# A two-layer encoder trunk: another order for the gate stage and the query and key projections, and feed-forward work moved to GpSimd

## The chip, the cores and the metric

The kernel runs on one core of one Trainium2 chip. The metric is the device time of one launch in microseconds. Before the change the median of three runs is 1855.73 us (1855.55 to 1857.43).

TensorE (PE in the profile, PEld for its weight loads) multiplies matrices and writes only to PSUM, eight banks of 128 x 512 fp32. VectorE (DVE), ScalarE (ACT) and GpSimd (POOL) do the elementwise work; each of them takes its instructions strictly in the order in which they were queued. SyncE (SP) issues most DMAs, also in order.

## The reference, cut to what matters

Two requests (512 prompt tokens and 256 sample tokens) go through DEPTH = 2 layers with the same weights. A layer is a mixer and a convolutional gated feed-forward network, each followed by a residual sum and a layer norm:

```python
aq, ak, av, lq, lk, lv, lo, lg = _split_cols(x @ w_in)
att = _head_rmsnorm(_diff_attention(aq, ak, av, lam), att_g) * (1.0 - lam_init)
gates = lg + gate_bias            # log input and forget gates, forward and backward
h = _mlstm(q, k, v, ig_f, lf_f) + flipped _mlstm(..., ig_b, lf_b)
mixed = concat([att, sigmoid(lo) * _head_rmsnorm(h, lstm_g)])
x = _layer_norm(ALPHA * x + mixed @ w_out)
gate, up = split(x @ w_gu)        # 2816 columns each
conv = conv_b + sum(gp[:, j:j + S] * conv_w[j] for j in range(3))
x = _layer_norm(ALPHA * x + (gelu(conv) * up) @ w_down)
```

Everything is fp32. The mLSTM needs, per head and direction, running sums and running maxima over the tokens of its gates, and exponentials of them, before it can form any state.

## The kernel before, in words

The 768 tokens are six tiles of 128; tiles 0 and 1 are the sample, tiles 2 to 5 the prompt. Activations lie transposed in `actA`, each value split into a high and a low part. A product takes three passes over the parts (`PASSES`), so one 128 x 512 output tile over 1024 inputs is 24 matmuls. Weights come by DMA into six raw buffers (`_load`, L140), ACT makes the high part (L171) and DVE the low part (L172), into 12 slots (`Weights`). `take` hands out the next block, `done` gives its slot back and plans the next conversion.

**Order of the work.** Python generators write the instructions down. `weave` (L739) advances several generators in turn: it always picks the one with the smallest (steps done + 0.5) / n, where n is the number given beside it. The place at which an instruction is written is its priority; a planner then fills each engine's queue. At every moment of its own estimate it takes the instruction of highest priority that it believes ready. So a matmul written early can stand behind later ones in the queue if the planner thought its inputs late. On the chip the queue is kept as it is: an instruction at its head whose input is late holds up all behind it.

**Gates, per layer.** After `lstm_in`, `gates()` (L428) runs beside `dense("av")`, the value projection of the attention (six tiles of 24 matmuls). Its chain: logarithms on DVE and ACT up to `gs` (L461), transposes `gT` on PE (L474), scans on DVE (L483 to L487), sums and differences, an exponential on ACT (L509) and one of a small tile `ae` (L514), a product `aB` of `ae` on PE (L517), and four groups of transposes `colT` (L524). Two of its results go through DRAM (`scr_m`, `scr_e`) and come back broadcast over all partitions: `lstm_decay` loads `pt` (L570), adds a mask on DVE (L572) and takes exponentials on ACT (L574).

**Query and key projections.** `att_in(h)` (L666) takes two weight blocks each for the query and the key of a head. `feat_major` (L347) runs 24 weight tiles; for each it multiplies the sample's 256 tokens into `psB` and the prompt's 512 into `psA`. Query and key of one head share the PSUM bank `aqkB` for the sample. Then ACT and DVE split the result into `sQ` (L678 to L681) or `sK` and `kL` (L683 to L688). `att(h)` (L692) does the scores (L708, L709), softmax and value product, sample first for heads 0 to 2. The value projection of the mLSTM, `dense("lv")`, is woven with `att(0)`.

**Feed-forward.** The 22 feature tiles (`ff_tile`, L924) use a scheme of seven products instead of eight (`product`, 12 matmuls of 384 columns each; p1, p2, p4, p6, p7, p5, p3 in this order). It needs four combinations of weight tiles, T1 to T4: T1 = u0 - g0 and T3 = u1 - u0 on GpSimd, T2 = u1 - T1 and T4 = T2 - g1 on VectorE (L149, planned at L299 to L302); each has one buffer, which becomes free when its conversion is done. The seven PSUM results are combined by DVE into the gate half `g` and the `up` half; the convolution, GELU and product with `up` (L954 to L964) follow. After the first tile of a group, `down` (L966) multiplies the three (last: four) tiles of the group before with `w_down`, in two PSUM banks by turns, and DVE adds each result to `acc` (L988). There are seven groups per layer; the last `down` uses three other banks.

Of the kernel before, what the change touches and what calls it, by code (L numbers as in the profile page):

```python
# [13 lines left out]
F32 = mybir.dt.float32  # L14
F32R = mybir.dt.float32r
AF = mybir.ActivationFunctionType
ALU = mybir.AluOpType
# [3 lines left out]
SA, SB = 512, 256  # L21
T = SA + SB
# [11 lines left out]
HALF = T // 2  # L34
# [12 lines left out]
PR_A = 0  # L47
PR_L = 0
PR_LO = 10
# [156 lines left out]
def trunk(ctx, nc, tc, d, o, depth=DEPTH):  # L206
    V, S, G, PE = nc.vector, nc.scalar, nc.gpsimd, nc.tensor
# [18 lines left out]
    def P(tag, name):  # L226
        return pp.tile([128, 512], F32, tag=tag, name=name, bufs=banks[tag])

    actA = cp.tile([128, 8, 2, T], F32R, name="actA")
# [17 lines left out]
    for i in range(2):  # L247
        k = 4 * i
# [17 lines left out]
    for l in range(depth):  # L266
        if l:
            for u in range(4):
                W.unit(d["w_c1"][l, u], 1056)
        for u in range(4):  # L270
            W.unit(d["w_av"][l, u])
        for h in range(4):
            W.unit(d["w_aq"][l, h])
            W.unit(d["w_ak"][l, h])
            if h == 0 or h == (1 if L1 else 2):
                for u in range(4):
                    W.unit(d["w_lv" if h == 0 else "w_lo"][l, u])
        for hf in range(2):
            for u in range(4):
                W.unit(d["w_out"][l, hf, u])  # L280
        early = {}
        for i in range(FF_EARLY):
            early[i] = [W.piece(d["w_g"][l, i, :, p * 512:(p + 1) * 512], 512) for p in range(2)]
            for src in early[i]:
                W.block(src, 512)
        for kind, i in ffn_seq:
            if kind == "f":

                def half(w, p):
                    return W.piece(d[w][l, i, :, p * 512:(p + 1) * 512], 512)  # L290

                if i in early:
                    g0, g1 = early[i]
                else:
                    g0, g1 = half("w_g", 0), None
                u0, u1 = half("w_u", 0), half("w_u", 1)
                if g1 is None:
                    g1 = half("w_g", 1)
                t1 = {"a": u0, "b": g0, "tag": "T1", "engine": G}  # L299
                t2 = {"a": u1, "b": t1, "tag": "T2", "engine": V}  # L300
                t3 = {"a": u1, "b": u0, "tag": "T3", "engine": G}
                t4 = {"a": t2, "b": g1, "tag": "T4", "engine": V}  # L302
                for src in (t4, t2, t3, t1, u1) if i in early else (g0, g1, t4, t2, t3, t1, u1):
                    W.block(src, 512)
            else:
                f0, f1 = FF_GROUPS[i]
                for hf in range(2):
                    for f in range(f0, f1):
                        W.block(W.piece(d["w_down"][l, f, :, hf * 512:(hf + 1) * 512], 512), 512)
# [29 lines left out]
    PASSES = ((0, 0), (0, 1), (1, 0))  # L339
# [6 lines left out]

    def feat_major(blocks, psA, psB):  # L347

        n = 0
        for k in range(8):  # L350
            _, h, l = blocks[k // 4]
            for a, b in PASSES:
                w = (h, l)[a][:, (k % 4) * 128:(k % 4 + 1) * 128]
                PE.matmul(psB, w, actA[:, k, b, 0:SB], start=n == 0, stop=n == 23)  # L354
                PE.matmul(psA, w, actA[:, k, b, SB:T], start=n == 0, stop=n == 23)  # L355
                n += 1

    def transposed_split(src, name, tag, hi, lo):

# [8 lines left out]
    for l in range(depth):  # L368
# [3 lines left out]
        av = ra.tile([128, NT, 512], F32, name="av")  # L372
# [24 lines left out]
        def dense(tag, evac):  # L397
            units = [W.take() for _ in range(8)]
            for t in range(NT):
                p = P("d", f"{tag}{t}")  # L400
                tok_major(t, units, p, slice(0, 512))
                evac(t, p)
                yield
            W.done(*units)
# [23 lines left out]
        def gates():  # L428
            GP = ExitStack()
            gp = GP.enter_context(tc.tile_pool(name=f"gp{l}", bufs=1, reuse_waits="tile"))  # L430
            t1 = gp.tile([128, T], F32, name="t1")
# [5 lines left out]
            for di in range(2):  # L437
                for pr in range(2):
                    for hh in range(2):
                        s = sel[:, di * 2 + pr, hh * 64:(hh + 1) * 64]  # L440
                        G.affine_select(out=s, in_=s, pattern=[[0, 64]], compare_op=ALU.not_equal, fill=1.0, base=-(di * 32 + pr * 2 + hh), channel_multiplier=1)
            f = gt[:, :, :, 1, :]
            g1 = gp.tile([128, NT, 2, 4], F32, name="g1")
# [12 lines left out]
                                   in1=g1.rearrange("p a b c -> p (a b c)"), op0=ALU.add, op1=ALU.subtract)  # L456
# [10 lines left out]
            t2 = gp.tile([128, T], F32, name="t2")  # L467
            mpe = gp.tile([64, 2, 6], F32, name="mpe")
            ae = gp.tile([64, 6], F32, name="ae")
            for c0, c1 in ((0, 4), (4, 6)):  # L470
                ps = P(TAG_GT, f"gT{c0}")
                n = (c1 - c0) * 128
                for t in range(c0, c1):
                    PE.transpose(ps[:, (t - c0) * 128:(t - c0 + 1) * 128], gs[:, t].rearrange("p a b c -> p (a b c)"), ident)  # L474
                S.copy(ig[:, c0 * 128:c1 * 128], ps[0:64, :n])
                V.tensor_copy(lf[:, c0 * 128:c1 * 128], ps[64:128, :n])
# [35 lines left out]
            V.tensor_tensor(out=v6(t2[64:128]), in0=v6(t1[0:64]), in1=me.unsqueeze(2).to_broadcast([64, 6, 128]), op=ALU.subtract)  # L512
            V.tensor_tensor(out=ae, in0=mp, in1=me, op=ALU.subtract)
            S.activation(ae, ae, AF.Exp)  # L514
            ps = P(TAG_GT, "aB")
            for i in range(4):
                PE.matmul(ps[:, i * 6:(i + 1) * 6], sel[:, i, :], ae, start=True, stop=True)  # L517
# [221 lines left out]
        def weave(*gens):  # L739

            live = [[0, n, i, g, (*o, 0)[0]] for i, (g, n, *o) in enumerate(gens)]
            while live:
                e = min(live, key=lambda e: ((e[0] + 0.5) / e[1], e[2]))
                e[0] += 1
                with prio(e[4]):
                    done = next(e[3], live) is live
                if done:
                    live.remove(e)

        def chain(*gens):  # L750
            for g in gens:
                yield from g
# [3 lines left out]
            late_constants()  # L756
        G.iota(dneg, [[-1, 896]], base=384, channel_multiplier=1, allow_small_or_imprecise_dtypes=True)
        V.scalar_tensor_tensor(out=dneg, in0=dneg, scalar=-1.0, in1=dneg, op0=ALU.mult, op1=ALU.min)
        weave((gates(), 8), (dense("av", ev_av), 7))
        CPX = ExitStack()  # L760
        lc = CPX.enter_context(tc.tile_pool(name=f"lc{l}", bufs=1, reuse_waits="tile"))
        weave((att_in(0), 3))
        weave((att(0), 7, PR_A), (dense("lv", ev_lv), 7, PR_LO))
        lo = dense("lo", ev_lo)
        weave((chain(att_in(1), att(1)), AT1, PR_A), (chain(lstm_states(lc), *[lstm_out(lc, c) for c in range(OUTS)]), 4 * OUTS + 9, PR_L), *([(islice(lo, L1), L1 + W1)] if L1 else []))
        weave((chain(att_in(2), att(2)), AT2, PR_A), (chain(*[lstm_out(lc, c) for c in range(OUTS, NT)]), 4 * (NT - OUTS) + 1, PR_L), *([(islice(lo, L2), L2 + W2, PR_LO)] if L2 else []))
# [157 lines left out]
        def ff_tile(f):  # L924
            w0, w1, w2, cb = (convw[:, l, f, i:i + 1] for i in range(4))
            g = ft.tile([128, T], F32, tag="g", name=f"g{f}")
            up = ft.tile([128, T], F32, tag="up", name=f"up{f}")
            c = ft.tile([128, T], F32, tag="c", name=f"c{f}")
            m1, u2, u3, u4 = (ft.tile([128, HALF], F32, tag=t, name=f"{t}_{f}") for t in ("m1", "u2", "u3", "u4"))
            lo_, hi_ = slice(0, HALF), slice(HALF, T)  # L930
            p1 = bank(f"p1_{f}")
            product(p1, A11)
            S.copy(m1, p1)
            p2 = bank(f"p2_{f}")
            product(p2, A12)
            yield
            V.tensor_tensor(out=g[:, lo_], in0=p2, in1=m1, op=ALU.add)
            p4 = bank(f"p4_{f}")
            product(p4, A22)
            p6 = bank(f"p6_{f}")  # L940
            product(p6, S2)
            V.tensor_tensor(out=u2, in0=p6, in1=m1, op=ALU.add)
            p7 = bank(f"p7_{f}")
            product(p7, S3)
            V.tensor_tensor(out=u3, in0=p7, in1=u2, op=ALU.add)
            V.scalar_tensor_tensor(out=g[:, hi_], in0=p4, scalar=-1.0, in1=u3, op0=ALU.mult, op1=ALU.add)  # L946
            p5 = bank(f"p5_{f}")
            product(p5, S1)
            V.tensor_tensor(out=u4, in0=p5, in1=u2, op=ALU.add)
            V.tensor_tensor(out=up[:, hi_], in0=p5, in1=u3, op=ALU.add)  # L950
            p3 = bank(f"p3_{f}")
            product(p3, S4)
            V.tensor_tensor(out=up[:, lo_], in0=p3, in1=u4, op=ALU.add)
            S.activation(c, g, AF.Identity, bias=cb, scale=w1)  # L954
            for a, b in ((0, SB), (SB, T)):
                V.scalar_tensor_tensor(out=c[:, a + 1:b], in0=g[:, a:b - 1], scalar=w0, in1=c[:, a + 1:b], op0=ALU.mult, op1=ALU.add)
                V.scalar_tensor_tensor(out=c[:, a:b - 1], in0=g[:, a + 1:b], scalar=w2, in1=c[:, a:b - 1], op0=ALU.mult, op1=ALU.add)
            S.activation(c, c, AF.Gelu)
            V.tensor_tensor(out=up, in0=up, in1=c, op=ALU.mult)
            s = f % RING  # L960
            for half, sl in ((0, lo_), (1, hi_)):
                hi, lo = hm_half(s, 0, half), hm_half(s, 1, half)
                S.activation(hi, up[:, sl], AF.Identity)
                V.tensor_tensor(out=lo, in0=up[:, sl], in1=hi.bitcast(F32), op=ALU.subtract)  # L964
# [133 lines left out]
```

## Time and profile before

| | before |
|---|---|
| median of 3 runs | 1855.73 us |
| profiled execution | 1855.45 us, span 1853.7 us |
| granted TensorE clock, mean | 0.992 |
| PE busy | 1804.3 us (97%) |
| DVE, ACT, POOL busy | 1340.4 us (72%), 768.9 us (41%), 241.9 us (13%) |
| gate stage and first head, layer 1 | about 45 to 117 us of the span |
| the same, layer 2 | about 967 to 1036 us |
| feed-forward, layers 1 and 2 | about 436 to 904 us, 1355 to 1810 us |

The span runs from the first to the last instruction. Busy time is summed by engine; a wait is the idle time of an engine just before an instruction, put down to what released it. A granted clock of 1.00 is 2.4 GHz, one of 0.50 is 1.2 GHz.

### The profile page before, as it was taken

What the parts mean: (1) busy time and instruction counts of PE and PEld (TensorE: products, weight loads), DVE (VectorE), ACT (ScalarE), POOL (GpSimd) and SP (SyncE); (2) the same over time, 40 slices, a digit from 0 to 9 for tenths busy, and PEclk for the clock granted to TensorE, in tenths of its full rate; (3) what the DMA queues carried; (4) which work ended last, traced back from release to release, by engine and by line L of the source; (5) the groups of instructions that cost most, each with busy time, mean ns of one, the idle gap of its engine ahead of it and who ended that gap; (6) DMA issues with size and microseconds to landing.
All of it is one profiled execution on the core that took longest, in us unless ns stands there. A gap on an engine that the chain in (4) does not pass through costs nothing.

```text
span 1853.7 us, 26256 instructions
## 1 busy us (share of the span) xinstructions
PE 1804.3 (97%) x9692; PEld 1587.1 (86%) x9692; DVE 1340.4 (72%) x2576; ACT 768.9 (41%) x1624; POOL 241.9 (13%) x260
## 2 busy tenths in 40 slices
PE   8899999999999999999998999999999999999998
PEld 8778777789899899899897787777898998998996
DVE  5434787589887786787954457775898877877878
ACT  4344576425343343343332455672353343343340
POOL 2000111041111111110120011011411111111102
PEclk9999999999999999999999999999999999999999
DMA  6232110402322222122322121104022221221211
GB/s 190 67 79 69 35 58 24 159 18 69 92 74 69 64 74 68 64 75 86 101 96 83 42 69 52 46 25 170 2 90 80 80 79 47 80 76 51 80 63 68
DMA packets 83280, 134.95 MB, mean 73 GB/s; under 512 B 7984, under 2 KB 27056, under 8 KB 83152
## 3 DMA queue, kind: packets, MB, share of 16 engines
q1 hardware_dynamic: 82432, 132.90, 22.7%
q8 instruction: 76, 1.25, 0.3%
q14 instruction: 52, 0.43, 0.1%
q10 hardware_dynamic: 720, 0.37, 0.1%
HBM read 126.86 MB, written 6.39 MB: 72 GB/s over the span
## 4 chain that ended last, share of the span: by engine, by line
PE 78%; DVE 13%; ACT 5%; issue 2%; POOL 2%; DMA 1%; SPq 0%; DVEq 0%; ACTq 0%; POOLq 0%
PE p L921 32%; PE dn L981 16%; PE wo L877 5%; PE aqkA L355 3%; PE lv L345 3%; PE lo L345 3%; PE aqkB L354 2%; DVE wl L172 2%; PE c1a L345 2%; PE u L724 2%; PE av L345 2%; PE c1b L345 2%; PE num L618 1%; ACT wh L171 1%; PE num L614 1%
## 5 line engine op out<-in xcount | busy, mean ns | idle before, releaser
L921 PE MATMUL p<-actA,wh 128*128 128x384 f32 x1408 | 363.4, 338 | 3.2 <-DVE g L946 3.2
L171 ACT ACTIVATE wh<-raw 128x512 fp32r<-128x512 f32 (+1 forms) x348 | 215.5, 629 | 303.3 <-PE p L921 110.2
L172 DVE TENSOR_TENSOR wl<-raw,wh 128x512 fp32r<-128x512 f32 (+1 forms) x348 | 243.2, 708 | 96.9 <-ACT wh L171 96.4
L921 PE MATMUL p<-actB,wh 128*128 128x384 f32 x1056 | 270.0, 337 | 0.0
L921 PEld LDWEIGHTS p<-actA,wh 128*128 128x128 f32 x1408 | 254.7, 188 | 5.8 <-DVE g L946 3.8
L921 PE MATMUL p<-actA,wl 128*128 128x384 f32 x704 | 237.3, 337 | 0.0
L149 POOL TENSOR_TENSOR T<-raw,raw 128x512 f32<-128x512 f32 x88 | 120.5, 1371 | 837.0 <-DVE wl L172 525.7
L981 PE MATMUL dn<-wh,actB 128*128 128x512 f32 x576 | 208.8, 396 | 1.1 <-DVE acc L988 1.1
L171 ACT ACTIVATE wh<-T 128x512 fp32r<-128x512 f32 x176 | 108.4, 628 | 221.3 <-DVE acc L988 104.9
L921 PEld LDWEIGHTS p<-actB,wh 128*128 128x128 f32 x1056 | 191.3, 188 | 0.0
L981 PE MATMUL dn<-wh,ring 128*128 128x512 f32 x480 | 179.1, 396 | 1.6 <-DVE acc L988 1.6
L921 PE MATMUL p<-actB,wl 128*128 128x384 f32 x528 | 177.2, 336 | 0.0
L988 DVE TENSOR_TENSOR acc<-acc,dn 128x512 f32<-128x512 f32 x144 | 98.1, 681 | 72.0 <-PE dn L981 71.7
L172 DVE TENSOR_TENSOR wl<-T,wh 128x512 fp32r<-128x512 f32 x176 | 129.6, 748 | 22.0 <-ACT wh L171 21.9
L981 PEld LDWEIGHTS dn<-wh,actB 128*128 128x128 f32 x576 | 108.0, 188 | 29.8 <-DVE acc L988 2.8
L921 PEld LDWEIGHTS p<-actA,wl 128*128 128x128 f32 x704 | 132.2, 188 | 0.1
L877 PE MATMUL wo<-wh,actB 128*128 128x512 f32 x384 | 122.7, 396 | 0.0
L981 PE MATMUL dn<-wl,actB 128*128 128x512 f32 x288 | 113.2, 393 | 0.0
L981 PEld LDWEIGHTS dn<-wh,ring 128*128 128x128 f32 x480 | 90.0, 188 | 24.6 <-DVE acc L988 4.2
L921 PEld LDWEIGHTS p<-actB,wl 128*128 128x128 f32 x528 | 99.1, 188 | 0.0
L355 PE MATMUL aqkA<-actA,wh 128*128 128x512 f32 x256 | 98.8, 408 | 0.0
L981 PE MATMUL dn<-wl,ring 128*128 128x512 f32 x240 | 94.5, 394 | 0.0
(265 smaller groups left out, 3412.5 us busy)
## 6 DMA issues: line engine op xcount, KB each, us to landing
raw<-in_w_g_dram SPq DMA_DIRECT2D x88, 256.0 KB, 2.8
raw<-in_w_u_dram SPq DMA_DIRECT2D x88, 256.0 KB, 2.8
raw<-in_w_down_dram SPq DMA_DIRECT2D x88, 256.0 KB, 2.8
raw<-in_w_out_dram SPq DMA_DIRECT2D x32, 256.0 KB, 2.6
pt<-scr_m SPq DMA_DIRECT2D x12, 512.0 KB, 6.2
raw<-in_w_c_dram SPq DMA_DIRECT2D x16, 264.0 KB, 3.6
raw<-in_w_av_dram SPq DMA_DIRECT2D x16, 256.0 KB, 4.1
raw<-in_w_aq_dram SPq DMA_DIRECT2D x16, 256.0 KB, 3.7
```

The lines of the kernel that those rows point to most:

```text
L149: src["engine"].tensor_tensor(out=src["tile"], in0=a, in1=b, op=ALU.subtract)
L171: self.nc.scalar.activation(h, v, AF.Identity)
L172: self.nc.vector.tensor_tensor(out=l, in0=v, in1=h.bitcast(F32), op=ALU.subtract)
L345: PE.matmul(ps, xh(k, t, a), (h, l)[b][:, cols], start=k + i == 0, stop=k == 7 and i == 2)
L354: PE.matmul(psB, w, actA[:, k, b, 0:SB], start=n == 0, stop=n == 23)
L355: PE.matmul(psA, w, actA[:, k, b, SB:T], start=n == 0, stop=n == 23)
L614: PE.matmul(pn[:, di * 256:di * 256 + 129], qet[r, di, hh // 2, :], cst[di, c][r, hh // 2, :], start=di == dirs[0], stop=False, skip_group ...
L724: PE.matmul(pu[:, qt * 128:(qt + 1) * 128], aT[:, st * 128:(st + 1) * 128], av[:, s0 + st, h * 128:(h + 1) * 128], start=st == 0, stop=st ...
L877: PE.matmul(p, actB[:, k, a, t * 128:(t + 1) * 128], units[k][1 + b], start=n + i == 0, stop=n == 7 and i == 2)
L921: PE.matmul(ps, blk[1 + a][:, k * 128:(k + 1) * 128], x[:, k, b, :], start=k + i == 0, stop=k == 3 and i == 2)
L981: PE.matmul(p, x, (wh_, wl_)[b], start=k + i == 0, stop=k == nf - 1 and i == 2)
L988: V.tensor_tensor(out=z, in0=z, in1=p, op=ALU.add)
```

## The change

Four edits. (1) `gates()` gets two more yields, before the `gT` transposes and before the `aB` product, and is woven in ten steps with a longer chain: the value projection, `att_in(0)`, and the first tile of `lv`. The separate step for `att_in(0)` goes, and `att(0)` is woven with the five tiles of `lv` that remain. (2) `feat_major` does all 24 matmuls of the sample, then all 24 of the prompt; this holds for all four heads. (3) T2 and T4 are computed on GpSimd. (4) In `ff_tile` ACT copies p5 to the SBUF tile `m5`, and GpSimd adds it to `u2` (in place) and to `u3` (into the second half of `up`), where DVE did both from PSUM.

```diff
-                t2 = {"a": u1, "b": t1, "tag": "T2", "engine": V}
+                t2 = {"a": u1, "b": t1, "tag": "T2", "engine": G}
                 t3 = {"a": u1, "b": u0, "tag": "T3", "engine": G}
-                t4 = {"a": t2, "b": g1, "tag": "T4", "engine": V}
+                t4 = {"a": t2, "b": g1, "tag": "T4", "engine": G}
...
-        n = 0
-        for k in range(8):
-            _, h, l = blocks[k // 4]
-            for a, b in PASSES:
-                w = (h, l)[a][:, (k % 4) * 128:(k % 4 + 1) * 128]
-                PE.matmul(psB, w, actA[:, k, b, 0:SB], start=n == 0, stop=n == 23)
-                PE.matmul(psA, w, actA[:, k, b, SB:T], start=n == 0, stop=n == 23)
-                n += 1
+        for ps, tok in ((psB, slice(0, SB)), (psA, slice(SB, T))):
+            n = 0
+            for k in range(8):
+                _, h, l = blocks[k // 4]
+                for a, b in PASSES:
+                    w = (h, l)[a][:, (k % 4) * 128:(k % 4 + 1) * 128]
+                    PE.matmul(ps, w, actA[:, k, b, tok], start=n == 0, stop=n == 23)
+                    n += 1
...
             ae = gp.tile([64, 6], F32, name="ae")
+            yield
             for c0, c1 in ((0, 4), (4, 6)):
...
             S.activation(ae, ae, AF.Exp)
+            yield
             ps = P(TAG_GT, "aB")
...
-        weave((gates(), 8), (dense("av", ev_av), 7))
+        lv = dense("lv", ev_lv)
+        weave((gates(), 10), (chain(dense("av", ev_av), att_in(0), islice(lv, 1)), 10))
         CPX = ExitStack()
         lc = CPX.enter_context(tc.tile_pool(name=f"lc{l}", bufs=1, reuse_waits="tile"))
-        weave((att_in(0), 3))
-        weave((att(0), 7, PR_A), (dense("lv", ev_lv), 7, PR_LO))
+        weave((att(0), 7, PR_A), (lv, 6, PR_LO))
...
-            V.tensor_tensor(out=u4, in0=p5, in1=u2, op=ALU.add)
-            V.tensor_tensor(out=up[:, hi_], in0=p5, in1=u3, op=ALU.add)
+            S.copy(m5, p5)
+            G.tensor_tensor(out=u2, in0=m5, in1=u2, op=ALU.add)
+            G.tensor_tensor(out=up[:, hi_], in0=m5, in1=u3, op=ALU.add)
...
-            V.tensor_tensor(out=up[:, lo_], in0=p3, in1=u4, op=ALU.add)
+            V.tensor_tensor(out=up[:, lo_], in0=p3, in1=u2, op=ALU.add)
```

## Rows read from the trace of the kernel before

**Rows 1.** The page, part 1: busy time of each engine, share, instructions.
```profile
PE 1804.3 (97%) x9692; PEld 1587.1 (86%) x9692; DVE 1340.4 (72%) x2576; ACT 768.9 (41%) x1624; POOL 241.9 (13%) x260
```

**Rows 2.** PE's waits, whole span: instruction <- releaser: total us, times, longest us.
```profile
PE aB L517 <- ACT ae L514: 10.5, 2, 5.3
...
PE aqkB L354 <- DVE sQ L681: 5.8, 2, 3.4
PE p L921 <- DVE g L946: 3.2, 2, 1.6
PE dn L981 <- DVE acc L988: 2.7, 10, 0.3
...
PE s L708 <- ACT sK L685: 1.8, 2, 0.9
```

**Rows 3.** Timeline of PE, both layers' gate stages: start, us, instruction, [idle before <- releaser].
```profile
45.19 0.40 PE L345 MATMUL av<-wh,actA 128*128 128x512 f32 x1
...
50.55 0.63 PE L474 MATMUL gT<-ident,gs 128*128 128x128 f32 x4 [0.80 <-DVE gs L461]
...
67.11 1.84 PE L517 MATMUL aB<-ae,sel 64*128 64x6 f32 x8 [5.26 <-ACT ae L514]
...
966.81 0.39 PE L345 MATMUL av<-wh,actA 128*128 128x512 f32 x1
...
973.25 0.63 PE L474 MATMUL gT<-ident,gs 128*128 128x128 f32 x4 [1.16 <-DVE gs L461]
...
989.80 1.84 PE L517 MATMUL aB<-ae,sel 64*128 64x6 f32 x8 [5.25 <-ACT ae L514]
```

**Rows 4.** Windows: length, then busy of PE, PEld, DVE, ACT, POOL; PEclk; DMA share; GB/s.
```profile
67.10:73.00 5.90, 5.89 (x19) 5.00 (x20) 0.18 (x1) 0.31 (x1) 0.00 (x0) 0.51 0.02 6
...
104.30:108.00 3.70, 3.66 (x14) 3.38 (x15) 3.27 (x5) 1.82 (x5) 0.00 (x0) 0.50 0.09 8
108.00:117.00 9.00, 8.86 (x41) 7.13 (x40) 2.23 (x4) 6.05 (x16) 0.00 (x0) 0.86 0.23 77
...
989.80:995.00 5.20, 5.20 (x19) 4.54 (x20) 0.18 (x1) 0.77 (x2) 0.00 (x0) 0.55 0.02 5
...
1024.80:1028.00 3.20, 3.19 (x13) 2.97 (x14) 2.84 (x5) 1.79 (x5) 0.00 (x0) 0.57 0.01 4
```

**Rows 5.** Chain of work that ended last: start, us, piece (24 and 252 matmuls).
```profile
73.28 5.55 PE av L345 x24
...
500.30 43.97 PE p L921 x252
```

**Rows 6.** The same chain, then ACT's timeline, from 93 to 103 us.
```profile
93.04 7.22 DMA pt<-scr_m
...
101.16 1.57 ACT L574 ACTIVATE pt<-pt,cols 128x128 f32<-128x128 f32 x5 [5.72 <-DVE pt L572]
102.64 0.36 ACT L678 ACTIVATE sQ<-aqkB 64x256 fp32r<-64x256 f32 x1
```

**Rows 7.** Groups by line and shape, 500 to 904 us: busy us, mean ns | idle before.
```profile
L172 DVE TENSOR_TENSOR wl<-raw,wh 128x512 fp32r<-128x512 f32 x87 | 59.1, 685 | 6.8 <-ACT wh L171 6.8
...
L149 DVE TENSOR_TENSOR T<-raw,T 128x512 f32<-128x512 f32 x16 | 10.9, 682 | 8.5 <-POOL T L149 8.5
...
L950 DVE TENSOR_TENSOR up<-p,u 128x384 f32<-128x384 f32 x18 | 9.8, 547 | 0.0
...
L149 POOL TENSOR_TENSOR T<-raw,raw 128x512 f32<-128x512 f32 x32 | 42.4, 1326 | 321.1 <-DVE wl L172 200.8 <-DMA raw<-in_w_u_dram 90.8 <-DVE g L946 21.7
```

**Rows 8.** Window of the feed-forward of layer 1, columns as in rows 4.
```profile
500.00:904.00 404.00, 402.68 (x2105) 374.46 (x2104) 313.82 (x513) 152.36 (x248) 44.26 (x34) 1.00 0.23 73
```

**Rows 9.** DVE's timeline inside one `down`, one of six like it.
```profile
563.57 0.69 DVE L988 TENSOR_TENSOR acc<-acc,dn 128x512 f32<-128x512 f32 x1 [1.38 <-PE dn L981]
```

**Rows 10.** POOL's and DVE's timelines at the start of the feed-forward of layer 1.
```profile
429.38 3.39 POOL L149 TENSOR_TENSOR T<-raw,raw 128x512 f32<-128x512 f32 x2 [6.19 <-DVE wl L172]
...
429.82 4.10 DVE L172 TENSOR_TENSOR wl<-raw,wh 128x512 fp32r<-128x512 f32 x3
```

More of the change, by code (lines that the diff above doesn't have):

```diff
@@ L928, in ff_tile @@
             c = ft.tile([128, T], F32, tag="c", name=f"c{f}")
-            m1, u2, u3, u4 = (ft.tile([128, HALF], F32, tag=t, name=f"{t}_{f}") for t in ("m1", "u2", "u3", "u4"))
+            m1, u2, u3, m5 = (ft.tile([128, HALF], F32, tag=t, name=f"{t}_{f}") for t in ("m1", "u2", "u3", "m5"))
             lo_, hi_ = slice(0, HALF), slice(HALF, T)
```

## The prediction, made before the changed kernel was run

> **What bounds the kernel now.** I read the busy times first: TensorE is busy for 1804.3 us of a span of 1853.7 [rows 1], so at most 49 us of idle time can be won, and whatever PE loses by a slower clock. Work taken off another engine is worth only what PE waits for it. So I read PE's waits next [rows 2]. Two stand out, both once per layer in the gate stage: `aB` waits 10.5 us in all for ACT's `ae`, and `aqkB` 5.8 us for DVE's `sQ`. The feed-forward, half of the span, has next to none: 3.2 us at its two starts and 2.7 us in ten pieces in `down`. Then PE's timeline and the windows round the two big waits: `aB` starts after 5.26 and 5.25 us of idle [rows 3], and in the 5.9 and 5.2 us after it PE is granted 0.51 and 0.55 of its clock, the lower of its levels (1.2 GHz) for most of the time; after the `aqkB` wait it is 0.50, then 0.86, and 0.57 in layer 2 [rows 4]. So each of these waits is paid twice, as idle time and as slow matmuls.
>
> Durations are from one execution of 1855.45 us, whose span is 1853.7 us; the sum is made against 1855.45. The median of the three runs is 0.3 us higher. A difference within 0.2% (3.7 us) is one that a measurement of this kernel cannot tell from none.
>
> **Gates and `aB`.** By the weave's rule the gates (eight steps) wrote `aB` third, ahead of the third value tile; PE met it in the middle of that tile, before its input was there. With ten steps against ten, the order is: value tile 0, `gT`, tile 1, scans, tile 2, `ae`, tile 3, `aB`, tile 4, then one `colT` after each of tile 4, tile 5, the query and the key. I take it that PE keeps this order, since everything written ahead is ready. A value tile takes 5.55 us [rows 5]. Layer 1: tiles start at 45.19 [rows 3]; four of them and the six `gT` transposes (0.5 us, estimated from the 0.63 us of a row of four) end at 67.9 us. `aB` could start at 67.11; `gT` comes 0.2 us later than before (at the end of tile 0, 50.74, and not at 50.55), so at 67.3. Covered, by 0.6 us. Layer 2: tiles start at 966.81, tile 0 ends at 972.36, `gT` still waits until 973.25, and `aB` comes at 990.4 against 989.80 before. Covered too, by 0.6 us; what the margin lacks on the chip would be lost again, one for one.
> So the 10.5 us go. Of the 1.96 us before `gT` some 0.9 stay in layer 2: 1.1 us go. Clock: 5.9 x 0.49 + 5.2 x 0.45 = 5.2 us; but 1.84 us of each window are the tiny `aB` products, for which half the time is no more than a bound, so between 3.4 and 5.2: I take 4.3 us.
>
> **Sample first.** Query and key of a head share the bank `aqkB`, so the key's sample matmuls wait until the query's sample result is evacuated. Interleaved, sample and prompt end together; now the sample's 24 end a whole prompt run (24 matmuls of 512 columns, 5.55 us as a value tile [rows 5]) before the key's begin. The evacuation took from 102.64 us [rows 6] to PE's restart at 104.3 [rows 4]: 1.7 us, well inside 5.55. The 5.8 us go, and with them the slow matmuls: 3.7 x 0.50 + 9.0 x 0.14 + 3.2 x 0.43 = 4.5 us. The scores' wait of 1.8 us for `sK` goes too: the key's sample is evacuated under the prompt's matmuls, and the first `lv` tile stands between. Matmuls and weight loads stay the same in number. The first block of each pair is held for half a sample run more, about 1.4 us (12 matmuls of half a value matmul's width); the next conversions have 12 slots and no PE wait names them, so nothing.
>
> **What comes late next.** `att_in(0)` moves ahead of the last `colT`, and so the load of `pt`, which waited for the gate tiles' space, moves back behind the key. That load stands on SP behind raw loads, takes 7.22 us, and ACT, in order, sat 5.72 us at `pt` with the `sQ` evacuations behind it [rows 6]: this is why `sQ` was late at all. Now the first softmax of `att(0)` may stand behind `pt` on DVE and ACT. The load and the exponentials take 7.22 + 1.57 = 8.8 us; the `lv` tile covers 5.55. Left are 3.2 us per layer, and matmuls of the next `lv` tile cover a part. Bounds: 0, and the whole of the old price, 10.3 us. I take 2 us per layer, 4 in all, nearer to zero because PE now has work in that place. `att(0)` has one `lv` tile fewer beside it; `att_in(1)` is next and its matmuls need only a free bank, so nothing.
>
> **Feed-forward.** Per feature tile DVE loses T2 and T4 and two additions: 2 x 0.682 + 2 x 0.547 = 2.5 us of work [rows 7]. POOL gains 2 x 1.326 [rows 7] and two additions of 384 columns, 0.99 us each if they scale (up to 1.7, what each of two T tiles took in [rows 10]): 4.6 us. It was busy 44.26 us in a window of 18 tiles [rows 8], 2.5 us each, and comes to 7.1 of the 22.4 us that a tile with its share of `down` takes. ACT gains a copy, some 0.5 us from the 0.36 of 256 columns [rows 6], and is 38% busy. PE was busy for 402.7 of 404 us, so relief for DVE is worth at most the two waits, 5.9 us.
> The new wait is `up` (L953) and the product with `up` (L959) on DVE for POOL. Behind them on DVE stand the additions of `down` (L988), the conversions and the next tile's results. A product is 12 matmuls, 43.97 / 21 = 2.09 us [rows 5]: from p5's end POOL has this long before p3 ends. Copy 0.5 and addition 0.99 fit in; if a T subtraction is under way, 1.3 us more make L953 about 0.7 us late. DVE has 90 us of slack in the 404, 5.0 per tile. So I take 0, with bounds -5.9 and, for POOL's queue in the wrong order, +32 (below).
>
> **A rule that speaks against it.** While POOL ran two T subtractions in 3.39 us, three low-part conversions took 4.10 us [rows 10] where 3 x 0.685 = 2.06 are usual [rows 7]: 2 us lost to the overlap. At the two starts of the feed-forward, where PE does wait for DVE [rows 2], two more subtractions lengthen that overlap by as much again; less the DVE work that leaves that stretch, 0 to 2.7 us per layer. I take 0, since 2.5 us of DVE work per tile leave at the same time.
> The Trainium skill, "SBUF — State Buffer", section "Who interferes with whom", says that a VectorE instruction with two SBUF inputs and a GpSimd instruction that reads SBUF exclude each other for their full length. By that rule the loss is certain wherever they meet; the row agrees, its lost time being near to one subtraction and a half.
>
> **Sum.** 10.5 + 1.1 + 4.3 + 5.8 + 4.5 + 1.8 = 28.0 us less; 4.0 come back behind `pt`: 24.0. 1855.45 - 24.0 = 1831.5 us, and the 0.3 us to the median change nothing.
>
> **The rivals.**
> *The `pt` load moves its whole price.* For it: both engines are in order, and the planner once before put `pt` too early. Against: an `lv` tile lies between. 10.3 in place of 4.0: 1837.8 us. Chance 0.20.
> *POOL and DVE collide at the start of the feed-forward.* For: the 4.10 us row. Against: DVE has less to do. 2 x 2.7 = 5.4 us: 1836.9 us. Chance 0.12.
> *`aB` is not moved in fact.* The planner sets PE's queue by its own estimates, and it had put `aB` 5 us too early; were a value tile's bank thought late, `aB` would come ahead of it again. 10.5 + 4.3 come back: 1846.3 us. Against: three banks, whose value tiles were never late. Chance 0.06.
> *The small waits go too*, those of the feed-forward (5.9) and the 4 behind `pt`: 1821.6 us. Chance 0.07.
> *Slower: POOL's queue is late for the additions.* If the planner puts a run of four subtractions (4 x 1.33 = 5.3 us) ahead of a tile's additions, L953 comes 0.5 + 5.3 + 0.99 - 2.09 = 4.7 us late. DVE stands, and with it L988. `down` uses two banks, one result every 2.07 us [rows 9], so PE stands for 2.6 us, in 12 `down` calls (six per layer that follow the first tile of a group): 31.6 us, 1863 us. It makes the change slower from 2.0 us per call on (24.0 / 12). For: subtractions are planned 12 blocks ahead and start as soon as their buffers are free. Against: additions have the higher priority, and one wait is only as long as what already runs. Chance 0.10.
>
> **How the numbers follow.** The forecast has the remaining 0.45. Faster by over 0.2%: the forecast, the first four rivals (0.90), less some 0.04 for losses in the re-planned stretches that I cannot price, so 0.86; slower is most of the last rival, 0.09; no difference 0.05. The range goes from the best case, 1821, to 1850, past the case with `aB` in its old place; the last rival is left out, with little else.
>
> **What would show it.** After the change: no idle before `aB` and `aqkB`, and a granted clock of 1.00 from 45 to 117 us; `s` without a wait. `pt` on ACT after the key's evacuations; a PE wait at `aT` behind it is the price that I put at 4 us. In the feed-forward PE busy as before, DVE less, POOL at about a third, no wait of PE at `dn` above the present 0.3 us. I am wrong if `aB` or `aqkB` still wait, or if PE waits at `dn` for DVE that waits for POOL.

## The result: slower, 1923.94 us, and where the time is in the profile

The changed kernel takes 1923.94 us (median of 4 runs, 1921.75 to 1925.63) against 1856.58 us for the kernel before (4 runs): ratio 1.0362 [1.0344, 1.0380], some 67 us slower. The forecast was 1831.5 us, the range 1821 to 1850.

Busy times of the changed kernel (the page, part 1), to be held against [rows 1]:

```profile
PE 1824.0 (95%) x9692; PEld 1601.2 (83%) x9692; DVE 1375.0 (71%) x2400; ACT 782.6 (41%) x1668; POOL 502.2 (26%) x436
```

DVE has 176 instructions fewer than before and is busy for 35 us more: its instructions have become longer on average. PE executes the same 9692 matmuls in 20 us more. Then PE's waits, to be held against [rows 2] (columns as there):

```profile
PE dn L984 <- DVE acc L991: 42.4, 10, 4.5
PE p L923 <- DVE g L939: 9.9, 2, 5.7
...
PE dn L984 <- DVE acc L989: 6.9, 2, 3.5
PE p L923 <- DVE g L948: 4.3, 2, 2.9
PE p L923 <- ACT m L935: 3.5, 2, 1.8
...
PE dn L984 <- ACT actB L966: 2.4, 2, 1.4
```

`aB` and `aqkB` are gone from the list, as forecast. In their place stand waits of the feed-forward: `dn` for `acc`, 10 times, up to 4.5 us each, and `p` for `g` at its start. The groups of `down` and the first product with `w_out` in the chain of work that ended last give the place in time (start, us, piece; the changed kernel):

```profile
327.68 45.20 PE wo L879 x195
...
480.04 23.87 PE dn L984 x90
...
857.60 22.71 PE dn L984 x90
```

Of the kernel before, the same chain (its row at 500.30 us is in [rows 5]):

```profile
340.85 45.21 PE wo L877 x195
...
848.19 44.02 PE p L921 x252
```

Its row of `wo` stands at 340.85 us: the first layer of the changed kernel is 13.2 us ahead when its feed-forward comes near. From there it loses: five periods of `down` take 857.60 - 480.04 = 377.6 us, 75.5 each, where five of before take 848.19 - 500.30 = 347.9 us, 69.6 each.

Why a `down` is late is seen inside one. DVE of the kernel before, second full `down` of layer 1 (start, us, instruction, [idle before <- releaser]):

```profile
543.13 1.14 DVE L956 SCALAR_TENSOR_TENSOR c<-g,convw,c 128x255 f32<-128x255 f32 x2
...
544.76 1.14 DVE L957 SCALAR_TENSOR_TENSOR c<-g,convw,c 128x255 f32<-128x255 f32 x2
545.82 0.69 DVE L172 TENSOR_TENSOR wl<-T,wh 128x512 fp32r<-128x512 f32 x1
546.42 0.68 DVE L988 TENSOR_TENSOR acc<-acc,dn 128x512 f32<-128x512 f32 x1
547.02 1.67 DVE L959 TENSOR_TENSOR up<-up,c 128x768 f32<-128x768 f32 x1
```

The same stretch of the changed kernel, DVE, then POOL, then PE:

```profile
548.38 1.97 DVE L959 SCALAR_TENSOR_TENSOR c<-g,convw,c 128x255 f32<-128x255 f32 x2 [1.16 <-ACT c L957]
550.27 1.23 DVE L960 SCALAR_TENSOR_TENSOR c<-g,convw,c 128x255 f32<-128x255 f32 x1
...
551.90 0.73 DVE L960 SCALAR_TENSOR_TENSOR c<-g,convw,c 128x511 f32<-128x511 f32 x1
552.56 1.28 DVE L172 TENSOR_TENSOR wl<-T,wh 128x512 fp32r<-128x512 f32 x2
553.76 2.01 DVE L962 TENSOR_TENSOR up<-up,c 128x768 f32<-128x768 f32 x1
555.70 0.68 DVE L991 TENSOR_TENSOR acc<-acc,dn 128x512 f32<-128x512 f32 x1
```

```profile
548.79 1.02 POOL L952 TENSOR_TENSOR u<-m,u 128x384 f32<-128x384 f32 x1 [6.25 <-ACT m L951]
549.76 1.47 POOL L953 TENSOR_TENSOR up<-m,u 128x384 f32<-128x384 f32 x1
553.37 3.54 POOL L149 TENSOR_TENSOR T<-raw,raw 128x512 f32<-128x512 f32 x2 [2.14 <-issue]
```

```profile
556.43 0.79 PE L984 MATMUL dn<-wh,ring 128*128 128x512 f32 x1 [4.38 <-DVE acc L991]
```

The convolution starts just when POOL makes the two additions, and is stretched; the product L962 meets two subtractions. From the first step of the convolution to the first addition of `down` DVE needs 7.3 us (548.38 to 555.70), before it was 3.3 us. Much of these 4.0 us is order: the planner now puts this addition behind the product L962 (1.9 us, itself stretched) and not ahead of it, and behind one conversion more (0.6 us); the longer convolution is the other 1.5 us. PE fills its two banks, stands for 4.38 us, and goes on slowly (a window, columns as in [rows 4]):

```profile
556.40:560.00 3.60, 3.57 (x8) 2.81 (x9) 3.07 (x3) 0.35 (x1) 3.44 (x3) 0.50 0.25 75
```

0.50 is the lower clock, 1.2 GHz: as in the gate stage of before, each wait is paid twice.

Over the feed-forward of layer 1 (500 to 904 us, groups by line and shape: busy us, mean ns), the conversions and the convolution before and after:

```profile
L956 DVE SCALAR_TENSOR_TENSOR c<-g,convw,c 128x511 f32<-128x511 f32 x18 | 14.4, 803 | 0.0
...
L957 DVE SCALAR_TENSOR_TENSOR c<-g,convw,c 128x255 f32<-128x255 f32 x18 | 10.5, 582 | 0.0
```

```profile
L172 DVE TENSOR_TENSOR wl<-raw,wh 128x512 fp32r<-128x512 f32 x81 | 64.7, 814 | 8.7 <-ACT wh L171 8.7
...
L959 DVE SCALAR_TENSOR_TENSOR c<-g,convw,c 128x511 f32<-128x511 f32 x16 | 24.8, 1550 | 0.0
...
L960 DVE SCALAR_TENSOR_TENSOR c<-g,convw,c 128x255 f32<-128x255 f32 x16 | 19.7, 1233 | 0.0
```

One step of the convolution goes from 803 to 1550 ns, one from 582 to 1233, a conversion from 685 [rows 7] to 814 (about five per tile, 0.63 us). With the other stretched rows of the same groups (the two other steps 194 and 171 ns, the product 130, the two subtractions L967 that form the low parts of a tile's result 235 each, the conversions of T tiles 16 each) that is about 3.05 us more per tile, where 2.5 us of DVE work left. (Rows of before for these: 492, 744, 1150, 656 on average, 727; after: 686, 915, 1280, 891, 743.) What did not become longer are DVE's instructions with one operand in PSUM: the additions of `down` take 685 ns against 682, and those that combine products 544 to 554 against 547 to 558. POOL's own work was undersized too: its T subtractions went from 1326 ns to 1524 to 1551, and the two additions took 1075 and 1465 ns instead of 0.99 us each.

### The profile page after: what moved, and what is told of

It is laid out like the page before. It is cut to its first block, busy times and chain, and to the rows that moved or that the text cites. A ratio compares the mean times of both kernels' runs of the same rounds, so it can differ in the third digit from the quotient of the medians.

```text
span 1923.9 us, 26411 instructions
## 1 busy us (share of the span) xinstructions
PE 1824.0 (95%) x9692; PEld 1601.2 (83%) x9692; DVE 1375.0 (71%) x2400; ACT 782.6 (41%) x1668; POOL 502.2 (26%) x436
## 4 chain that ended last, share of the span: by engine, by line
PE 71%; DVE 15%; issue 5%; ACT 4%; POOL 4%; DMA 1%; SPq 0%; POOLq 0%; DVEq 0%; ACTq 0%
PE p L923 22%; PE dn L984 16%; PE wo L879 5%; PE aqkA L355 4%; DVE wl L172 4%; PE av L345 3%; PE lo L345 2%; PE lv L345 2%; DVE c L960 2%; PE aqkB L355 2%; DVE up L962 2%; PE u L726 2%; PE c1a L345 2%; PE c1b L345 2%; DVE c L959 1%
## 5 line engine op out<-in xcount | busy, mean ns | idle before, releaser
L923 PE MATMUL p<-actA,wh 128*128 128x384 f32 x1408 | 368.0, 340 | 7.9 <-DVE g L948 4.3
L172 DVE TENSOR_TENSOR wl<-raw,wh 128x512 fp32r<-128x512 f32 (+1 forms) x348 | 267.5, 784 | 69.1 <-ACT wh L171 68.6
L149 POOL TENSOR_TENSOR T<-raw,raw 128x512 f32<-128x512 f32 x88 | 135.0, 1541 | 514.6 <-DVE wl L172 283.6
L984 PE MATMUL dn<-wh,actB 128*128 128x512 f32 x576 | 217.7, 412 | 26.4 <-DVE acc L991 17.1
L984 PE MATMUL dn<-wh,ring 128*128 128x512 f32 x480 | 185.7, 411 | 25.3 <-DVE acc L991 25.3
L923 PEld LDWEIGHTS p<-actB,wh 128*128 128x128 f32 x1056 | 193.4, 190 | 10.6 <-DVE g L939 10.6
L984 PEld LDWEIGHTS dn<-wh,actB 128*128 128x128 f32 x576 | 113.8, 198 | 56.3 <-DVE acc L991 19.0
L984 PEld LDWEIGHTS dn<-wh,ring 128*128 128x128 f32 x480 | 94.1, 196 | 49.9 <-DVE acc L991 28.4
L959 DVE SCALAR_TENSOR_TENSOR c<-g,convw,c 128x255 f32<-128x255 f32 x88 | 89.0, 1052 | 46.4 <-ACT c L957 46.4
L984 PE MATMUL dn<-wl,actB 128*128 128x512 f32 x288 | 117.8, 409 | 0.0
L952 POOL TENSOR_TENSOR u<-m,u 128x384 f32<-128x384 f32 x44 | 49.4, 1122 | 199.1 <-ACT m L951 198.9
```

The source lines that it names most:

```text
L149: src["engine"].tensor_tensor(out=src["tile"], in0=a, in1=b, op=ALU.subtract)
L172: self.nc.vector.tensor_tensor(out=l, in0=v, in1=h.bitcast(F32), op=ALU.subtract)
L923: PE.matmul(ps, blk[1 + a][:, k * 128:(k + 1) * 128], x[:, k, b, :], start=k + i == 0, stop=k == 3 and i == 2)
L952: G.tensor_tensor(out=u2, in0=m5, in1=u2, op=ALU.add)
L984: PE.matmul(p, x, (wh_, wl_)[b], start=k + i == 0, stop=k == nf - 1 and i == 2)
```

## The experiments

Theory A: GpSimd's instructions that read SBUF lengthen DVE's instructions with two SBUF inputs; PE meets this as waits for `acc` and `g`. Theory B: the moved work itself, as copy, wait for POOL or re-planned order, is late, and overlap costs little. In each experiment the time of the kernel before was measured on the same chip; its medians were 1856.8 to 1857.6 us.

**Gate stage alone: edits (1) and (2).** The feed-forward is that of before.

```diff
-                t2 = {"a": u1, "b": t1, "tag": "T2", "engine": G}   # and T4
+                t2 = {"a": u1, "b": t1, "tag": "T2", "engine": V}
-            G.tensor_tensor(out=u2, in0=m5, in1=u2, op=ALU.add)
+            V.tensor_tensor(out=u4, in0=p5, in1=u2, op=ALU.add)
```

> The two edits of the gate stage and of the projections alone; the feed-forward is as before. Both theories: all of the gain and none of the loss. From the start of the gate stage to the first product with w_out the changed kernel was about 13 us shorter in layer 1, so 1857 - 26 = about 1830 us, and PE's waits at dn as before (2.7 us in all). If it comes out above 1845, the gain seen in the gate stage is given back elsewhere.

1832.73 us (1832.09 to 1834.24), ratio 0.9870 [0.9855, 0.9884]. The half of the change that was forecast to gain does gain, 24.8 us by the medians. Its page, part 1, and the waits that are left in that stage:

```profile
PE 1795.7 (98%) x9692; PEld 1580.0 (86%) x9692; DVE 1343.0 (73%) x2576; ACT 768.7 (42%) x1624; POOL 242.0 (13%) x260
```

```profile
PE aT L722 <- DVE tp L719: 2.3, 2, 1.3
...
PE s L710 <- ACT sK L687: 1.1, 2, 0.6
```

**T2 and T4 on GpSimd alone: edit (3).**

```diff
-"tag": "T2", "engine": V      # T4 alike
+"tag": "T2", "engine": G
```

> T2 and T4 on GpSimd alone. Theory A (a DVE instruction with two SBUF inputs and a GpSimd instruction that reads SBUF stop each other): four subtractions in a row instead of two stretch DVE's conversions and convolution; about half of the loss of 93 us that the feed-forward showed, 1880 to 1905 us, with DVE instructions of two SBUF inputs longer on average (L957 on 255 columns above its 582 ns). Theory B (the queues were ordered for a shorter chain, and the new steps from ACT to GpSimd to DVE come late): no such chain here and DVE has less to do, so 1850 to 1858 us.

1879.94 us (1877.61 to 1880.48), ratio 1.0120 [1.0105, 1.0135]: 22 us slower, at the lower end of Theory A's range. PE's queue is almost that of before (by tile and shape, 9680 of 9692 matmuls in the same order), so there is little order in it. From 420 to 930 us L957 takes 1027 ns with 511 columns (before 743) and 619 with 255 (562), L964 into `ring` 1043 (665), a conversion of a raw tile 765 (720). A holds.

**Copy and two additions on GpSimd alone: edit (4).**

```diff
-            V.tensor_tensor(out=u4, in0=p5, in1=u2, op=ALU.add)
-            V.tensor_tensor(out=up[:, hi_], in0=p5, in1=u3, op=ALU.add)
+            S.copy(m5, p5)
+            G.tensor_tensor(out=u2, in0=m5, in1=u2, op=ALU.add)
+            G.tensor_tensor(out=up[:, hi_], in0=m5, in1=u3, op=ALU.add)
```

> The copy of p5 on ACT and the two additions on GpSimd alone; T2 and T4 stay on VectorE. Theory A: the additions run just when DVE does the convolution, so a loss in every tile, 30 to 60 us, 1887 to 1917 us, and the convolution's instructions are longer. Theory B: nearly the whole loss, 1930 to 1950 us, with DVE waiting for GpSimd at the sums and the product with up.

1911.33 us (1905.89 to 1919.31), ratio 1.0295 [1.0265, 1.0325]: 54 us slower. The convolution, by line and shape from 420 to 930 us:

```profile
L957 DVE SCALAR_TENSOR_TENSOR c<-g,convw,c 128x511 f32<-128x511 f32 x22 | 26.5, 1204 | 0.0
L958 DVE SCALAR_TENSOR_TENSOR c<-g,convw,c 128x255 f32<-128x255 f32 x22 | 24.9, 1132 | 0.0
```

DVE's wait for POOL's additions, which my slower rival needed, is this in all:

```profile
DVE up L954 <- POOL u L950: 1.7, 4, 0.4
```

**The copy on ACT, the additions on VectorE.** As the last, with V for G.

```diff
-            G.tensor_tensor(out=u2, in0=m5, in1=u2, op=ALU.add)   # the next line alike
+            V.tensor_tensor(out=u2, in0=m5, in1=u2, op=ALU.add)
```

> ACT copies p5 to m5 and VectorE, not GpSimd, does the two additions from m5; T2 and T4 stay on VectorE. Theory A: GpSimd does nothing new, so as before within 5 us, 1852 to 1862 us. Theory B: the copy alone makes the chain longer and brings another order; a third or more of the loss, above 1885 us.

1866.58 us (1865.87 to 1868.14), ratio 1.0053 [1.0037, 1.0070]: 9 us, of the 54, outside what either theory said. The copy and the re-planned order cost that; the other 45 us come with the two additions on GpSimd, a part of them perhaps by a further change of order. The convolution's steps of 511 columns are back at 742 and 745 ns. Theory B has its small part, A the large one.

**Two GpSimd additions that nobody waits for**, added to the kernel before. They change values that are not used again.

```diff
             V.tensor_tensor(out=up[:, hi_], in0=p5, in1=u3, op=ALU.add)
+            for _ in range(2):
+                G.tensor_tensor(out=u3, in0=u3, in1=u2, op=ALU.add)
```

> The kernel before, and in each feature tile GpSimd also does two additions of 384 columns on u3 after VectorE's last reading of it; nobody waits for their result, DVE and ACT do all that they did. Theory A (mutual exclusion of the two engines' SBUF reading): the same loss as from the real additions over the kernel in which VectorE did them from the copy (1911 - 1867 = 45 us), 1885 to 1905 us, the convolution on 255 and 511 columns longer by 0.3 to 0.5 us. Theory B (the steps from ACT to GpSimd to DVE come late): nothing waits here, so 1855 to 1862 us.

1892.54 us (1890.27 to 1894.26), ratio 1.0193 [1.0178, 1.0208]: 36 us for work on no path. Here order is no rival: compared by tile and shape, PE's 9692 matmuls stand in the order of before, and so do 2566 of DVE's 2576 instructions. POOL and DVE from 420 to 930 us:

```profile
L952 POOL TENSOR_TENSOR u<-u,u 128x384 f32<-128x384 f32 x44 | 53.1, 1207 | 148.2 <-DVE up L950 146.2
```

```profile
L958 DVE SCALAR_TENSOR_TENSOR c<-g,convw,c 128x511 f32<-128x511 f32 x22 | 32.6, 1481 | 0.0
...
L959 DVE SCALAR_TENSOR_TENSOR c<-g,convw,c 128x511 f32<-128x511 f32 x22 | 21.4, 974 | 0.0
```

**As much GpSimd time that only writes**: six memsets of the same tile.

```diff
+            for _ in range(6):
+                G.memset(u3, 0.0)
```

> The same place in each tile, but GpSimd only writes: six memsets of 384 columns into u3 in place of the two additions, about as long in all. If only reading by GpSimd stops DVE: 1855 to 1862 us and the convolution at its usual 0.56 and 0.74 to 0.79 us. If any GpSimd work in that place does it: the loss of the run with the two additions.

1859.64 us (1857.95 to 1861.11), ratio 1.0015 [1.0006, 1.0025]: 3 us, within what can be told from none.

```profile
L952 POOL MEMSET u<- 128x384 f32 x132 | 55.3, 419 | 148.4 <-DVE up L950 142.0
```

```profile
L958 DVE SCALAR_TENSOR_TENSOR c<-g,convw,c 128x511 f32<-128x511 f32 x22 | 16.4, 744 | 0.0
```

The same place in the program, the same GpSimd time per tile (55.3 against 53.1 us in a layer), and the convolution keeps its length. What stops DVE is that GpSimd reads. This is what the Trainium skill says, "SBUF — State Buffer", section "Who interferes with whom": a VectorE instruction with two SBUF inputs contends with a GpSimd instruction that reads SBUF, not with one that only writes it, over a port pair that only one of them can hold. The two runs agree, and give the size: 1481 against 744 ns, the difference more than half of an addition's 1207. That it takes two SBUF inputs, the changed kernel shows at the start of its feed-forward, DVE first, then POOL:

```profile
428.16 0.55 DVE L956 TENSOR_TENSOR up<-p,u 128x384 f32<-128x384 f32 x1
428.62 2.75 DVE L959 SCALAR_TENSOR_TENSOR c<-g,convw,c 128x255 f32<-128x255 f32 x2
431.30 3.14 DVE L960 SCALAR_TENSOR_TENSOR c<-g,convw,c 128x255 f32<-128x255 f32 x2
```

```profile
427.64 3.18 POOL L149 TENSOR_TENSOR T<-raw,raw 128x512 f32<-128x512 f32 x2
430.90 1.59 POOL L149 TENSOR_TENSOR T<-raw,T 128x512 f32<-128x512 f32 x1
```

L956, with `p` in PSUM, keeps its 0.55 us beside POOL's subtractions; the steps of the convolution right behind it take 2.75 and 3.14 us in pairs, where a pair took 1.14.

**The additions of `down` queued earlier**, in the changed kernel.

```diff
-                    V.tensor_tensor(out=z, in0=z, in1=p, op=ALU.add)
+                with prio(DN):      # DN = 400; the gi == 0 branch alike
+                    V.tensor_tensor(out=z, in0=z, in1=p, op=ALU.add)
```

> The changed kernel with one difference: the additions of down to acc get a priority of 400 instructions earlier, so that DVE does them ahead of conversions and of the product with up that are queued at the same time. If the loss reaches PE only by the first results of each down standing behind stretched DVE work (4.4 us of idle each, 12 times, and the slow matmuls after it): 1870 to 1890 us and waits at dn below 15 us in all. If DVE is late everywhere: above 1910 us, the wait only moves to another place.

1899.39 us (1897.62 to 1902.08), ratio 1.0227 [1.0210, 1.0244]: 25 us better than the changed kernel, 67 us worse than the gate stage alone, and between my two expectations (PE's waits at `dn` are 34.0 us in all, 51.7 in the changed kernel). The order gives back a quarter of the 91 us. DVE, same stretch:

```profile
549.62 0.68 DVE L993 TENSOR_TENSOR acc<-acc,dn 128x512 f32<-128x512 f32 x1
550.22 1.43 DVE L963 TENSOR_TENSOR up<-up,c 128x768 f32<-128x768 f32 x1
```

The first addition now stands ahead of the product, and PE's longest wait for it falls from 4.5 to 2.6 us. It still stands behind the stretched convolution (1448 and 1210 ns in the long steps), and the waits at the start of the feed-forward are as they were (`p` for `g`: 9.9 us).

**The longer weave alone: edit (1).**

```diff
             ae = gp.tile([64, 6], F32, name="ae")
+            yield
...
+        weave((gates(), 10), (chain(dense("av", ev_av), att_in(0), islice(lv, 1)), 10))
```

> The longer weave of the gate stage alone, query and key products interleaved as before. By the prediction's terms the wait before aB goes (10.5 + 1.1 + 4.3 us) and the wait of aqkB for the evacuation of the query's sample stays at a smaller price, since ACT has no load of pt in front of it: 1838 to 1845 us. If sample first brings nothing by itself: 1833 us as with both.

1832.98 us (1832.55 to 1833.75), ratio 0.9873 [0.9859, 0.9888]: all of the gain. I had priced the sample's order apart; but the weave also takes `pt` in ACT's queue from ahead of `sQ` to behind it, and with it the `aqkB` wait (0.4 us are left). ACT in this kernel:

```profile
90.17 0.63 ACT L171 ACTIVATE wh<-raw 128x512 fp32r<-128x512 f32 x1 [3.60 <-PE aqkA L355]
90.71 0.36 ACT L680 ACTIVATE sQ<-aqkB 64x256 fp32r<-64x256 f32 x1
...
105.70 0.70 ACT L576 ACTIVATE pt<-pt,cols 128x128 f32<-128x128 f32 x2 [1.95 <-issue]
```

**Sample first alone: edit (2).**

```diff
-            for a, b in PASSES:      # sample and prompt by turns
+            # all 24 of the sample, then all 24 of the prompt
```

> Sample first in the query and key products alone; gate stage as before. If the sample's early end lets its evacuation come before the load of pt, the aqkB wait goes (5.8 us of idle, 4.5 us of slow matmuls, and the 1.8 us before the scores): about 1845 us. If ACT has put pt in front of the sample's evacuation all the same, the wait stays: 1853 to 1858 us. With the weave alone at 1833 us and both at 1833 us, either way it adds nothing once the weave is changed.

1851.35 us (1848.92 to 1855.77), ratio 0.9969 [0.9959, 0.9979]: 6 us, between my two expectations. The `aqkB` wait goes here too, but `pt` is still early and part of it comes back: PE waits 4.3 us at `aT`, where it waited 0.2. So (1) and (2) cure one wait twice; together they gain what (1) gains.

**Both feed-forward edits without the gate stage: (3) and (4).**

```diff
-                t2 = {"a": u1, "b": t1, "tag": "T2", "engine": V}   # T4 alike
+                t2 = {"a": u1, "b": t1, "tag": "T2", "engine": G}
...
-            V.tensor_tensor(out=u4, in0=p5, in1=u2, op=ALU.add)
-            V.tensor_tensor(out=up[:, hi_], in0=p5, in1=u3, op=ALU.add)
+            S.copy(m5, p5)
+            G.tensor_tensor(out=u2, in0=m5, in1=u2, op=ALU.add)
+            G.tensor_tensor(out=up[:, hi_], in0=m5, in1=u3, op=ALU.add)
```

> Both feed-forward edits without the two early ones. If the two halves of the change do not touch each other, the loss is that of the whole change over the early edits alone, 1924 - 1833 = 91 us: 1857 + 91 = 1948 us. One by one the two feed-forward edits lose 22 + 54 = 76 us: 1933 us would say that 15 us come from their meeting the early edits, 1948 us that the two feed-forward edits make each other worse.

1949.12 us (1945.85 to 1954.29), ratio 1.0488 [1.0471, 1.0506]. The halves are independent: the two edits cost 1949.12 - 1857.64 = 91.5 us here and 1923.94 - 1832.73 = 91.2 us behind the other two. But singly they cost 22 + 54 = 76: together about 15 us more than their sum, with the 13 us that the runs of (4) alone spread over as its uncertainty.

**The other way: all four combinations on VectorE**, with the gate stage's two edits.

```diff
-                t1 = {"a": u0, "b": g0, "tag": "T1", "engine": G}   # T3 alike; T2 and T4 as before
+                t1 = {"a": u0, "b": g0, "tag": "T1", "engine": V}
```

> The two early edits, and all four weight combinations on VectorE: GpSimd then reads nothing in the feed-forward. DVE gains 1.4 us of work per feature tile and loses the stretching by GpSimd's two subtractions (the conversions and the product with up, 0.7 to 1.1 us against 0.68 and 0.95). If already the two subtractions cost something that PE sees: below 1830 us. If DVE's added work meets the first results of down: 1836 to 1860 us. PE has only 6 us of waits in the feed-forward to win.

1822.84 us (1820.46 to 1823.08), ratio 0.9811 [0.9797, 0.9826]: 10 us better than the gate stage alone, and the best version. DVE has more to do (busy 1357.7 us against 1343.0) and PE waits for it nowhere in the feed-forward (window of layer 1); the conversions and the product have their shortest times (420 to 930 us):

```profile
500.00:900.00 400.00, 400.00 (x2085) 370.85 (x2084) 321.43 (x543) 148.49 (x242) 4.39 (x6) 1.00 0.24 74
```

```profile
L172 DVE TENSOR_TENSOR wl<-raw,wh 128x512 fp32r<-128x512 f32 x108 | 73.2, 686 | 8.7 <-ACT wh L171 8.7
...
L961 DVE TENSOR_TENSOR up<-up,c 128x768 f32<-128x768 f32 x22 | 20.9, 950 | 0.0
```

A period of `down` is 69.1 us instead of 69.6. The two subtractions that stood on GpSimd before had a price as well: 6.2 us of PE's idle time and 3.0 of its busy time are gone. DVE's order is another one here, and no run parts its share from that of the shorter instructions.

## Why the prediction was wrong, step by step

**Bound (PE's waits and its clock): right.** It also accounts for the loss. Between the gate stage alone and the changed kernel PE's waits at the feed-forward rise from 6.0 us (3.2 + 2.8) to 69.4 (42.4 + 9.9 + 6.9 + 4.3 + 3.5 + 2.4), 63 us, and its busy time for the same matmuls, which is the clock, from 1795.7 to 1824.0, 28 us: together 91.7 of the 93.4 us by which the two profiled spans differ (1923.9 less 1830.5). The medians differ by 91.2.

**Gates and `aB`: right.** The `aB` product runs without idle time in front of it:

```profile
68.49 1.05 PE L519 MATMUL aB<-ae,sel 64*128 64x6 f32 x8
69.47 0.50 PE L345 MATMUL av<-wh,actA 128*128 128x512 f32 x1
```

The granted clock from 45 to 117 us is 1.00. Clock terms: 4.3 + 4.5 = 8.8 us forecast, 8.6 less PE busy time measured (1804.3 to 1795.7). Idle terms: 10.5 + 1.1 + 5.8 + 1.8 - 4.0 = 15.2 forecast; span less PE busy time fell from 49.4 to 34.8, 14.6 measured. Sum 24.0; the two spans differ by 23.2, the medians by 24.8 (1857.53 to 1832.73).

**Sample first: the wait goes, its share was not its own.** The 5.8 us and their clock belong to the weave as much; alone it brings 6 us. The wait of `s` went from 1.8 to 1.1 us, not to nothing: it stands at 305.7 and 1224.9 us in the kernel before, at the scores of the last head, where no `lv` tile lies between. The prediction read it as one of the first head.

**`pt` late: the mechanism was right, the size half.** It shows where it was forecast, at `aT`: 2.3 us for both layers in place of 0.2, where 4 were put. (The waits at `aoT` rose by 2.1 us as well, from 1.0 + 1.1 to 2.6 + 1.6; no run shows why.)

**Feed-forward: this step failed.** It said: "DVE has 90 us of slack in the 404, 5.0 per tile. So I take 0", and of the overlap, priced only at the two starts, "I take 0, since 2.5 us of DVE work per tile leave at the same time". Both are wrong, by 91 us together, where the highest bound was 32.
The row [rows 10] held the rate, 2 us lost against 3.39 us of POOL. I asked for it only where PE already waited. The two dummy additions show it in the middle of every tile: against the memsets, the four convolution groups of one layer last 28 us longer (32.6 + 21.4 + 17.0 + 14.5 against 16.4 + 16.3 + 11.4 + 13.2), and the kernel takes 33 us longer (1892.54 less 1859.64), 16 a layer. In the changed kernel the stretch (about 3.05 us per tile) is more than the relief (2.5).
And the slack was an average. DVE's idle time lies behind results of PE: 35 of the 90 us in `down`, in pieces of up to 1.4 us [rows 9], and 29 before results of the products; what is late is late at the beginning of `down`, where the convolution, its neighbours and the first additions stand in one queue and PE has only two banks ahead. The idle time that follows cannot be used backwards.
At the start of the feed-forward the same happens without `down`: four of the convolution's steps in 5.9 us (2.75 + 3.14), where before they take 2.28 (2 x 1.14), beside POOL that is busy nearly throughout. In the PE timelines the first `down` begins 144.5 us after the row of `wo` in the changed kernel (472.17 less 327.68) and 133.9 in the gate stage alone (461.82 less 327.92): 10.6 us later, and 11.7 us in layer 2. So some 22 of the 91 us are lost before any `down`.

**The rivals.** The slower one had the right victim (L988 late, PE standing at `dn`, in 12 `down` calls, 10 and 2 in the rows) and the wrong cause: DVE never waits for POOL's additions in the changed kernel, and the additions alone gave 1.7 us of such waits. DVE's instructions themselves become longer, which no list of waits shows. The collision rival had the right cause, but only a part of the place and a quarter of its price there: 5.4 us at the two starts, where some 22 were lost, and nothing for the other 69.

**Open.** Why (3) and (4) exceed their sum by some 15 us: later in the tile, POOL's additions may push its subtractions into DVE's product and low parts, as in the timeline above, but no run separates that. What of the 9 us of the copy is the copy and what the order: in that run VectorE's addition into `up` takes 651 ns in place of 546, and the convolution waits for ACT's `c` (0.95 us of idle time before it in each tile, none before). How much of the 67 us that remain with the earlier additions is order elsewhere.

## What to carry to other kernels

Before work is moved to GpSimd, list what DVE does at that moment with two SBUF operands, and price every overlap at a good part of GpSimd's time, not only those on the path; on an engine that works in order, average idle time is no cover for a delay that stands ahead of the result that is waited for. A move in the other direction may gain even though DVE gets busier: its instructions get shorter. Two edits that remove the same wait are worth it once; the weave alone gave all of the 24 us.

## What the runs showed of the hardware that was not expected

DVE's groups of before were already stretched: 1150 ns for the 768-column product and 727 for a conversion of a T tile, against 950 and 686 with GpSimd out of the feed-forward. A busy share says nothing of this: the added time counts as busy and not as a wait. Six GpSimd memsets per tile (419 ns each) cost the kernel no more than 3 us, two additions with the same total time 36.
